# A buffer of their own for added pieces, and a first residual spread over four pieces, in a macaron encoder block

## The chip, the cores and the metric

The kernel runs on 1 core of one Trainium2 chip. The metric is the device time of one execution in microseconds (us). Engines are named as in the profile: PE is TensorE (matmuls; PEld its weight loads), DVE is VectorE, ACT is ScalarE, POOL is GpSimd, SP is SyncE, which here only issues DMA transfers.

## The reference

One layer on 256 tokens of width 2048, all in float32; every norm is an RMS norm.

```python
x = x + 0.5 * swiglu(rms_norm(x, ffn1_norm), ffn1_w_up, ffn1_w_down)
h = rms_norm(x, mix_norm)
proj = h @ w_in            # HGRN2 q, f, i, g; RG-LRU branch and gate; two branch gates
...                        # y_a: chunked gated recurrence; y_b: conv(4), RG-LRU scan, gelu gate
x = x + (g_a * (y_a @ w_branch_a) + g_b * (y_b @ w_branch_b)) @ w_out
x = x + cross_attention(rms_norm(x, xattn_norm), rms_norm(mem, mem_norm), wq, wkv, wo)
x = x + 0.5 * swiglu(rms_norm(x, ffn2_norm), ffn2_w_up, ffn2_w_down)
return rms_norm(x, final_norm)

def swiglu(h, w_up, w_down):
    gate, up = jnp.split(h @ w_up, 2, axis=-1)     # w_up is 2048 x 11264, w_down 5632 x 2048
    return (jax.nn.silu(gate) * up) @ w_down
```

## The kernel before

All weights stream through SBUF once, in pieces of 128 x 2048 float32 (1 MB). A piece is loaded into a buffer `raw`, then split into a high part `h` (ACT rounds it to fp32r, line 120) and a low part `l` (DVE subtracts, line 121), so that each float32 product becomes three fp32r products of high and low parts: two lines of PE (449 and 450) with `h`, one (452) with `l`. `raw`, `h` and `l` have three buffers each.

The two feed-forward layers (`ffn1`, `ffn2`) go through 11 groups of 512 hidden columns, each in 8 up pieces `wu` (p0 to p7), with the down pieces `wd` between. `ffn_order()` sets the order. Up pieces come in three kinds. *Plain*: load and split. *Fast*: seven products in place of eight; DVE forms differences `td` of the piece's columns (lines 213 to 215), and these are split too (`h<-td`, `tl`). *Mixed*: eight products, split like a plain one, but from (group 3, p6) on as an *added* piece: `begin_added` loads it (line 190), ACT writes its negative copy to `l` (line 191), and a DMA from POOL's queue adds `raw` to `l` in place (line 192); later `prepare` writes `h` (line 200). This spares DVE the subtraction. Group 3 (order p1, p3, p0, p4, p2, p6, p5, p7) has one added piece, groups 4 to 10 have two each, so each layer has 15.

`weights()` walks one plan of all pieces and prepares two pieces ahead of the products. A buffer of a pool is written again only when its last reader is done, and SP's queue is first in, first out: a load that waits for a free `raw` buffer holds back all loads behind it. A scheduler of the framework places instructions on each engine by its own estimate of times, except on SP, ACT and DVE during the first eight pieces, where the program's order is kept (`in_turn`); loads may be hoisted ahead when their buffer is free.

At the start (pieces 0 to 7 of `ffn1`, group 0), `head` and `rest` hang small steps on the pieces: `head_x(p)` loads an eighth of x by features (`xf`), scales it (`xg`) and splits it (`xh`, `xl`); `head_residual` loads the residual `x` by tokens and takes its squares (`TokenSquares.add`, ACT, line 352, into a scratch tile `junk`); `head_rstd` forms the root and its reciprocal `rtok`, then calls Silu once so that its table is loaded; `sums1` forms sums and differences `xs` of `xg` that the fast and mixed products need as operands, and splits them (`xd`, `xh`). The first products are scaled by `rtok` in `ev` when group 0 ends.

The pool `raw` serves plain, fast and added pieces alike:

```python
def begin_added(src):
    raw = rawp.tile([P, 2048], F32, name="raw", tag="raw")
    l = lp.tile([P, 2048], F32R, name="l", tag="l")
    sp.dma_start(raw, src)
    act.activation(l, raw, ACT.Copy, scale=-1.0)
    nc.gpsimd.dma_start(l, raw, accum_op=ALU.add)
```

Of the kernel before, what the change touches and what calls it, by code (L numbers as in the profile page):

```python
# [8 lines left out]
F32 = mybir.dt.float32  # L9
# [4 lines left out]
P = 128  # L14
T = 256
# [46 lines left out]
def block_kernel(ctx: ExitStack, tc: tile.TileContext, xT, xin, memT, vec, gfin, bgate, lruw, wu1, wd1, win, wv,  # L62
                 wg, wab, wout, wq, wk, wvm, wo, wu2, wd2, out_):
    nc = tc.nc
    pe, dve, act, sp = nc.tensor, nc.vector, nc.scalar, nc.sync

    def pool(name, bufs, **kw):
        return ctx.enter_context(tc.tile_pool(name=name, bufs=bufs, **kw))

    const = pool("const", 1)  # L70
    rawp = pool("raw", 3)
# [3 lines left out]
    small = pool("small", 2)  # L75
    psum = pool("psum", 8, space=bass.MemoryType.PSUM)
    scoped = {}

    @contextmanager
    def scope(**pools):  # L80
        with ExitStack() as inner:
            for name, bufs in pools.items():
                scoped[name] = inner.enter_context(tc.tile_pool(name=name, bufs=bufs, reuse_waits="tile"))
            yield
            scoped.clear()
# [4 lines left out]
    def t1(name="t1"):  # L90
        return scoped["tmp"].tile([P, T], F32, name=name, tag="t1")

    def bank(name="acc"):
        return psum.tile([P, 512], F32, name=name, tag="acc")
# [17 lines left out]
    xt = [const.tile([P, 4 * T], F32, name=f"x{q}") for q in range(4)]  # L112
# [48 lines left out]
    head, rest = [], {}  # L161
# [3 lines left out]
    def weights(*key):  # L165
        while plan and len(ahead) < 2:
            i = next(planned)
            k, src, kind = plan.pop(0)
            if i == 0:
                in_turn.enter_context(tc.manual_schedule(engines={sp.engine, act.engine, dve.engine}))  # L170
            if i < len(head):
                head[i]()
            if plan and plan[0][2] == "added":
                begun.append(begin_added(plan[0][1]))
            ahead.append((k, prepare(src, kind, 4 if i < 4 else 1)))
            if i in rest:
                rest[i]()
            if i == 7:
                in_turn.close()
        k, w = ahead.pop(0)  # L180
        assert k == key, (k, key)
        return w
# [2 lines left out]

    def begin_added(src):

        raw = rawp.tile([P, 2048], F32, name="raw", tag="raw")
        l = lp.tile([P, 2048], F32R, name="l", tag="l")
        sp.dma_start(raw, src)  # L190
        act.activation(l, raw, ACT.Copy, scale=-1.0)
        nc.gpsimd.dma_start(l, raw, accum_op=ALU.add)
        return raw, l
# [77 lines left out]
    class Operands:  # L271
# [13 lines left out]
        def add(self, src, gain=None):  # L285
            t = self.new()
            if gain is None:
                act.activation(t[:, :T], src, ACT.Copy)
                dve.tensor_tensor(out=t[:, T:], in0=src, in1=t[:, :T].bitcast(F32), op=ALU.subtract)
            else:  # L290
                act.activation(t[:, :T], src, ACT.Copy, scale=gain)
                dve.scalar_tensor_tensor(out=t[:, T:], in0=src, scalar=gain, in1=t[:, :T].bitcast(F32),  # L292
                                         op0=ALU.mult, op1=ALU.subtract)
            return t
# [10 lines left out]
    class Squares:  # L305
# [2 lines left out]

        def add(self, src):
            if self.ss is None:  # L310
                self.ss = small.tile([P, T], F32, name="ss", tag="ss")
                act.activation(self.ss, src, ACT.Square)
            else:
                s = t1("sq")
                act.activation(s, src, ACT.Square)
                dve.tensor_tensor(out=self.ss, in0=self.ss, in1=s, op=ALU.add)

        def rstd(self):

            acc = bank()  # L320
            pe.matmul(acc[:, :T], ones, self.ss, start=True, stop=True)
            std = t1("std")
            act.activation(std, acc[:, :T], ACT.Sqrt, bias=eps, scale=1.0 / D)
            r = small.tile([P, T], F32, name="rstd", tag="rstd", bufs=3)
            dve.reciprocal(out=r, in_=std)
            return r

# [9 lines left out]
            return r  # L337


    FFN_POOLS = dict(wide=3, hd=1)  # L340

    class TokenSquares:

# [3 lines left out]

        def add(self, c, ts=range(2)):
            for t in ts:
                name = "hd" if "hd" in scoped else "tmp2"  # L350
                junk = scoped[name].tile([P, 512], F32, name="junk", tag=name)
                act.activation(junk, xt[c][:, t * 512:(t + 1) * 512], ACT.Square,
                               accum_out=self.ss[:, t * 4 + c:t * 4 + c + 1])

# [17 lines left out]
    def by_feature(r):  # L372

        diag = t1("diag")
        for t in range(2):
            dve.tensor_scalar(out=diag[:, t * P:(t + 1) * P], in0=ident, scalar1=r[:, t:t + 1], scalar2=None,
                              op0=ALU.mult)
        acc = bank()
        pe.matmul(acc[:, :T], ones, diag, start=True, stop=True)
        o = small.tile([P, T], F32, name="rstd", tag="rstd", bufs=3)  # L380
        act.activation(o, acc[:, :T], ACT.Copy)
        return o

# [187 lines left out]
    pairs1, sq1 = [], TokenSquares()  # L571
# [3 lines left out]
    def head_x(p):  # L575

        q = p // 2
        if p % 2 == 0:
            xq[q] = slot(name="xf"), slot(name="xg"), []
        src, xg, out = xq[q]  # L580
        a = p % 2 * 512
        sp.dma_start(src[:, a:a + 512], xT[:, p * 512:(p + 1) * 512])
        sums = operand_pairs([src[:, a:a + 512]], "ffn1_norm", q, xg, out)
        if p % 2:
            sums1.append(sums)
        pairs1.append(out[-1])

    def head_residual(i):
        for c in (2 * i, 2 * i + 1):
            for t in range(2):  # L590
                sp.dma_start(xt[c][:, t * 512:(t + 1) * 512], xin[t * P:(t + 1) * P, c * 512:(c + 1) * 512])
            sq1.add(c)
        if i:
            sp.dma_start(vt[:, small_n:NVEC], vec[:, small_n:])

    head += [lambda p=p: head_x(p) for p in range(8)]
    for i in range(2):
        rest[4 + i] = lambda i=i: head_residual(i)
    rstd1 = []

    def head_rstd():
        rstd1.append(sq1.rstd_tokens())
        act.activation(rstd1[0][:, 2:], rstd1[0][:, :1], ACT.Silu)

    for q, i in enumerate((3, 6, 7, 9)):
        rest[i] = lambda q=q: sums1[q](((0, "less"), (1, "sums")))
    rest[8] = head_rstd
    for q, i in ((1, 17), (2, 18)):
        rest[i] = lambda q=q: sums1[q](((0, "sums"),))

# [49 lines left out]

    with scope(**FFN_POOLS):
        ffn("ffn1", pairs1, sq1, to_mix, rstds=rstd1)

    middle = ExitStack()
    middle.enter_context(scope(tmp=8, tmp2=2, scores=1, extra=2))

    xs = xs2.tiles
    side = []
# [18 lines left out]
    def proj(i):  # L687
        acc = product(xs, weights("in", i), late2)
        if not rs:
            rs["t"] = sq2.rstd_tokens()  # L690
            rs["f"] = by_feature(rs["t"])
        return acc
# [280 lines left out]
    for m in range(KT):  # L973
        acc = product(xs3.tiles, weights("q", m), late)
        if m == 0:
            rstd = by_feature(sq3.rstd_tokens())
            dve.tensor_scalar(out=rstd, in0=rstd, scalar1=HD ** -0.5, scalar2=None, op0=ALU.mult)
        qs.add(summed(acc, by=rstd))
        for i in range(2 * m, 2 * m + 2) if m < 4 else (m + 4,) if m < 12 else ():
            if i % 4 == 0:  # L980
                mt = slot(name="mem")
                sp.dma_start(mt, memT[:, i * T:(i + 4) * T])
            mk = heads(mt)[:, i % 4]
            ms.add(mk, col("mem_norm", i))
            sqm.add(mk)
# [41 lines left out]
    for g in range(4):  # L1027
# [4 lines left out]
        for t in range(2):  # L1032
            s = slot(F32R, "vs")
            f = scoped["tmp2"].tile([P, 512], F32, name="vf", tag="part")
# [58 lines left out]

    with scope(**FFN_POOLS):
        ffn("ffn2", pairs2, sq4, to_out, late, sums2)
# [93 lines left out]
```

## Time and profile before

| what | value |
|---|---|
| median of 3 runs | 2455.01 us (2454.0 to 2455.87) |
| the profiled execution | 2456.57 us, span 2454.8 us |
| granted PE clock, mean | 0.997 |
| PE busy | 2434.6 us (99%), 12250 matmuls |
| DVE, ACT, POOL busy | 1894.1, 1391.2, 28.3 us |
| DMA | 507.59 MB, mean 207 GB/s |
| loads of one piece, issue to landing | 4.8 us, median of 172 up pieces |
| adding transfers on POOL's queue | 30, 7.3 us, median |

A row of a timeline gives start and duration in us, engine and line, the operation, the tiles as out<-in without buffer numbers, their shapes, how many were merged, and in brackets how long the engine had been idle and what ended that. Matmuls overlap: a row lasts 0.39 us and the next starts 0.23 us later. A windows row gives each engine's busy time in a stretch, the share of the clock that PE was granted, and what the DMA engines did.

### The profile page before, as it was taken

To read this page: it belongs to the slowest core of one execution; us is meant where nothing else is said; L and a number is where in the kernel's file an instruction comes from. 1 tells how busy PE (TensorE), PEld (TensorE's weight loads), DVE (VectorE), ACT (ScalarE), POOL (GpSimd) and SP (SyncE) were. 2 spreads that over 40 slices of the span, in tenths; PEclk is the share of its full clock that TensorE was granted. 3 is DMA by queue.
4 is the path that set the end of the run, shared out by engine and by line. 5 is a ranking of instruction groups with operands and counts; after the bars stand their busy time and mean duration, and the time that the engine had idled before them with its cause. 6 is when DMAs were issued, how large, how long until landed. Compare 5 with 4: busy or idle time off the path is not lost.

```text
span 2454.8 us, 30191 instructions
## 1 busy us (share of the span) xinstructions
PE 2434.6 (99%) x12250; PEld 2036.9 (83%) x12250; DVE 1894.1 (77%) x2016; ACT 1391.2 (57%) x1398; POOL 28.3 (1%) x36
## 2 busy tenths in 40 slices
PE   9999999999999999999999999999999999999998
PEld 7887888888888888888888888888888788888887
DVE  6998999999865757567665676556689999999995
ACT  7555666666564454477434554555555566666664
POOL 0000000000000000000000000000000000000000
PEclk9999999999999999999999999999999999999999
DMA  7557777777655445546555555444555677777774
GB/s 278 190 203 234 248 235 235 234 239 239 223 183 194 173 172 180 174 166 228 194 188 177 210 198 189 172 172 155 189 189 189 209 238 239 240 240 235 235 235 152
DMA packets 75020, 507.59 MB, mean 207 GB/s; under 512 B 8320, under 2 KB 8576, under 8 KB 15232
## 3 DMA queue, kind: packets, MB, share of 16 engines
q1 hardware_dynamic: 69840, 473.06, 53.4%
q0 software_dynamic: 4320, 31.46, 6.4%
q8 instruction: 96, 1.57, 0.2%
q10 hardware_dynamic: 720, 1.13, 0.1%
q14 instruction: 44, 0.36, 0.0%
HBM read 472.07 MB, written 2.10 MB: 193 GB/s over the span
## 4 chain that ended last, share of the span: by engine, by line
PE 95%; DVE 2%; ACT 1%; DMA 1%; issue 0%; SPq 0%; ACTq 0%; DVEq 0%
PE acc L449 17%; PE acc L450 17%; PE acc L452 17%; PE acc L231 11%; PE acc L252 8%; PE acc L253 8%; PE acc L255 8%; PE acc L235 5%; DMA raw<-wu 1%; PE acc L489 1%; ACT h L120 1%; DVE l L121 1%; PE acc L389 1%; PE acc L765 0%; PE acc L1048 0%; PE acc L1003 0%
## 5 line engine op out<-in xcount | busy, mean ns | idle before, releaser
L121 DVE TENSOR_TENSOR l<-raw,h 128x2048 fp32r<-128x2048 f32 (+2 forms) x422 | 878.0, 2087 | 364.5 <-ACT h L120 353.0
L120 ACT ACTIVATE h<-raw 128x2048 fp32r<-128x2048 f32 (+2 forms) x422 | 736.7, 1753 | 637.5 <-PE acc L253 204.8
L449 PE MATMUL acc<-h,xh 128*128 128x512 f32 x1280 | 501.2, 392 | 7.1 <-ACT h L120 7.0
L450 PE MATMUL acc<-h,xl 128*128 128x512 f32 x1280 | 499.7, 391 | 0.0
L120 ACT ACTIVATE h<-td 128x1024 fp32r<-128x1024 f32 x224 | 229.6, 1055 | 178.4 <-PE acc L450 131.0
L252 PE MATMUL acc<-h,ops 128*128 128x512 f32 x832 | 326.9, 393 | 0.0
L253 PE MATMUL acc<-h,ops 128*128 128x512 f32 x832 | 324.3, 390 | 0.0
L121 DVE TENSOR_TENSOR tl<-td,h 128x1024 fp32r<-128x1024 f32 x224 | 267.4, 1221 | 33.6 <-ACT h L120 31.0
L449 PEld LDWEIGHTS acc<-h,xh 128*128 128x128 f32 x1280 | 241.7, 189 | 60.0 <-ACT h L120 9.7
L450 PEld LDWEIGHTS acc<-h,xl 128*128 128x128 f32 x1280 | 241.9, 189 | 50.1
L231 PE MATMUL acc<-ops,h 128*128 128x512 f32 x1152 | 278.0, 393 | 0.3
L449 PE MATMUL acc<-h,hidop 128*128 128x512 f32 x704 | 275.7, 392 | 0.0
L450 PE MATMUL acc<-h,hidop 128*128 128x512 f32 x704 | 274.3, 390 | 0.0
L231 PEld LDWEIGHTS acc<-ops,h 128*128 128x128 f32 x1152 | 211.9, 188 | 42.9 <-DVE ops L292 0.9
L452 PE MATMUL acc<-l,xh 128*128 128x512 f32 x832 | 218.9, 390 | 0.0
L255 PE MATMUL acc<-l,ops 128*128 128x512 f32 x832 | 206.1, 390 | 0.0
L452 PE MATMUL acc<-l,hidop 128*128 128x512 f32 x704 | 188.3, 389 | 0.0
L452 PEld LDWEIGHTS acc<-l,xh 128*128 128x128 f32 x832 | 156.5, 188 | 32.6
L255 PEld LDWEIGHTS acc<-l,ops 128*128 128x128 f32 x832 | 156.2, 188 | 32.4
L252 PEld LDWEIGHTS acc<-h,ops 128*128 128x128 f32 x832 | 156.2, 188 | 32.3
L253 PEld LDWEIGHTS acc<-h,ops 128*128 128x128 f32 x832 | 156.3, 188 | 31.6
L452 PEld LDWEIGHTS acc<-l,hidop 128*128 128x128 f32 x704 | 132.2, 188 | 27.5
(220 smaller groups left out, 2347.6 us busy)
## 6 DMA issues: line engine op xcount, KB each, us to landing
raw<-wu SPq DMA_DIRECT2D x172, 1024.0 KB, 4.8
raw<-wd SPq DMA_DIRECT2D x88, 1024.0 KB, 4.8
raw<-win SPq DMA_DIRECT2D x40, 1024.0 KB, 4.8
raw<-wg SPq DMA_DIRECT2D x32, 1024.0 KB, 4.8
l<-raw POOLq DMA_DIRECT2D x30, 1024.0 KB, 7.3
raw<-wab SPq DMA_DIRECT2D x16, 1024.0 KB, 4.8
raw<-wout SPq DMA_DIRECT2D x16, 1024.0 KB, 4.8
raw<-wq SPq DMA_DIRECT2D x16, 1024.0 KB, 4.8
```

Source lines behind the costliest of these rows:

```text
L120: done["high"] = act.activation(h, raw, ACT.Copy).ins
L121: dve.tensor_tensor(out=l, in0=raw, in1=h.bitcast(F32), op=ALU.subtract)
L231: pe.matmul(acc, h[:, k * P:(k + 1) * P], xs[k], start=k == 0, stop=False)
L235: done["product"] = pe.matmul(acc[:, :T], l[:, k * P:(k + 1) * P], xs[k][:, :T], start=False, stop=k == KT - 1).ins
L252: pe.matmul(accs[t], x[:, t * P:][:, :P], h[j], start=first and j == 0, stop=False)
L253: pe.matmul(accs[t], x[:, T + t * P:][:, :P], h[j], start=False, stop=False)
L255: done["product"] = pe.matmul(accs[t], x[:, t * P:][:, :P], l[j], start=False, stop=last and j == 3).ins
L389: pe.transpose(accs[m // 2][:, m % 2 * T + t * P:][:, :P], tile[:, t * 512 + m * P:][:, :P], ident)
L449: pe.matmul(acc, ah, bh, start=start, stop=False)
L450: pe.matmul(acc, al, bh, start=False, stop=False)
L452: pe.matmul(acc, ah, bl, start=False, stop=stop)
L489: pe.transpose(acc[:, z * T + t * P:][:, :P], hid[t][:, (2 * y + z) * P:][:, :P], ident)
```

## The change

Four things change. `begin_added` loads into a tile `own` of a pool with one buffer (8 KB a partition), in place of one of the three `raw` buffers. For its space the scratch `hd` goes (the squares of the feed-forward layers write their `junk` into a `wide` tile), and `rstd` and `ss` move from `small` to a pool `feature` that lives only in the middle of the program. The first residual's loads and squares, two of its four quarters behind each of pieces 4 and 5 before, now come one quarter behind each of pieces 4, 5, 6 and 7. And `head_rstd` moves from behind the last of them to the next piece, with the sums around it moved by a piece or so. Core of the diff:

```diff
     def begin_added(src):
-        raw = rawp.tile([P, 2048], F32, name="raw", tag="raw")
+        raw = scoped["own"].tile([P, 2048], F32, name="own", tag="own")
...
-                self.ss = small.tile([P, T], F32, name="ss", tag="ss")
+                self.ss = scoped["feature"].tile([P, T], F32, name="ss", tag="ss", bufs=1)
...
-            r = small.tile([P, T], F32, name="rstd", tag="rstd", bufs=3)
+            r = scoped["feature"].tile([P, T], F32, name="rstd", tag="rstd")
...
-    FFN_POOLS = dict(wide=3, hd=1)
+    FFN_POOLS = dict(wide=3, own=1)
...
-                name = "hd" if "hd" in scoped else "tmp2"
-                junk = scoped[name].tile([P, 512], F32, name="junk", tag=name)
+                if "wide" in scoped:
+                    junk = scoped["wide"].tile([P, 2048], F32, name="junk", tag="wide")[:, :512]
+                else:
+                    junk = scoped["tmp2"].tile([P, 512], F32, name="junk", tag="tmp2")
...
-    def head_residual(i):
-        for c in (2 * i, 2 * i + 1):
-            for t in range(2):
-                sp.dma_start(xt[c][:, t * 512:(t + 1) * 512], xin[t * P:(t + 1) * P, c * 512:(c + 1) * 512])
-            sq1.add(c)
-        if i:
+    def head_residual(c):
+        for t in range(2):
+            sp.dma_start(xt[c][:, t * 512:(t + 1) * 512], xin[t * P:(t + 1) * P, c * 512:(c + 1) * 512])
+        sq1.add(c)
+        if c == 3:
             sp.dma_start(vt[:, small_n:NVEC], vec[:, small_n:])
...
-    for i in range(2):
-        rest[4 + i] = lambda i=i: head_residual(i)
...
-    for q, i in enumerate((3, 6, 7, 9)):
+    for i in range(3):
+        rest[4 + i] = lambda i=i: head_residual(i)
+    for q, i in enumerate((3, 7, 8, 9)):
         rest[i] = lambda q=q: sums1[q](((0, "less"), (1, "sums")))
-    rest[8] = head_rstd
+    made = rest[7], rest[8]
+    rest[7] = lambda: [f() for f in (lambda: head_residual(3), made[0])]
+    rest[8] = lambda: [f() for f in (head_rstd, made[1])]
...
-    middle.enter_context(scope(tmp=8, tmp2=2, scores=1, extra=2))
+    middle.enter_context(scope(tmp=8, tmp2=2, scores=1, extra=2, feature=3))
```

The first place is ACT's queue from the split of piece 5 (the first `h<-raw` row) to the first `ev`. `x_100`, `x_101` and `x_102` are quarters of the residual, `stdt` the root, `rtok` its reciprocal. Before:

```order
L120 ACTIVATE h<-raw 128x2048
L352 ACTIVATE junk,sst<-x_101 128x512 x2
L352 ACTIVATE junk,sst<-x_102 128x512 x2
L412 ACTIVATE xg<-xf,vt 128x256 x2
L362 ACT_TABLE_LOAD
L362 ACTIVATE stdt<-stdt,eps 128x2
L120 ACTIVATE xh<-xg 128x512
L603 ACT_TABLE_LOAD
L603 ACTIVATE rtok<-rtok 128x1
L120 ACTIVATE h<-raw 128x2048
```

And now, the split of piece 7 first, and between two such splits ahead of it only a pair of squares, `xg` and `xh`:

```order
L120 ACTIVATE h<-raw 128x2048
L354 ACTIVATE junk,sst<-x_102 128x512 x2
L120 ACTIVATE xd<-xs 128x256
L364 ACT_TABLE_LOAD
L364 ACTIVATE stdt<-stdt,eps 128x2
L120 ACTIVATE h<-raw 128x2048
L120 ACTIVATE xh<-xs 128x512
L602 ACT_TABLE_LOAD
L602 ACTIVATE rtok<-rtok 128x1
L120 ACTIVATE xd<-xs 128x256
L120 ACTIVATE xh<-xs 128x512
L483 ACTIVATE ev<-acc,rtok 128x512 x2
```

The two table loads have moved from ahead of the split of piece 6 to both sides of the split of piece 8, directly ahead of the first `ev`.

The second place is SP's queue at the start of the program (`xf` and `raw<-wu` are the loads of pieces 0, 1, 2 and so on, piece 2 being the third pair of rows). Before:

```order
L582 DMA xf<-xT 128x512
L207 DMA raw<-wu 128x512 x4
L582 DMA xf<-xT 128x512
L207 DMA raw<-wu 128x512 x4
L582 DMA xf<-xT 128x512
L207 DMA raw<-wu 128x512 x4
```

And now:

```order
L584 DMA xf<-xT 128x512
L207 DMA raw<-wu 128x512 x4
L584 DMA xf<-xT 128x512
L207 DMA raw<-wu 128x512 x4
L190 DMA own<-wu 128x2048
L584 DMA xf<-xT 128x512
L207 DMA raw<-wu 128x512 x4
```

The load of group 3's added piece has moved to the third place of the program, ahead of piece 2; in the same way the second layer's first one now stands among the loads of the cross-attention's value weights.

The third place is SP's queue from group 3's p0 to group 5 of the first layer; line 190 is an added piece's load, 210 a fast one's, 207 a plain one's or a down piece's. Before:

```order
L207 DMA raw<-wu 128x2048
L210 DMA raw<-wu 128x2048
L190 DMA raw<-wu 128x2048
L210 DMA raw<-wu 128x2048 x3
L207 DMA raw<-wd 128x2048 x4
L210 DMA raw<-wu 128x2048
L190 DMA raw<-wu 128x2048
L210 DMA raw<-wu 128x2048 x2
L190 DMA raw<-wu 128x2048
L210 DMA raw<-wu 128x2048 x3
```

And now:

```order
L207 DMA raw<-wu 128x2048
L210 DMA raw<-wu 128x2048 x4
L190 DMA own<-wu 128x2048
L207 DMA raw<-wd 128x2048 x4
L210 DMA raw<-wu 128x2048 x5
L190 DMA own<-wu 128x2048
L210 DMA raw<-wu 128x2048
L207 DMA raw<-wd 128x2048
L190 DMA own<-wu 128x2048
```

Group 3's four fast loads now stand in a row, and from group 4 on the first added piece of a group is loaded before the down pieces ahead of it, the second behind the group's fifth fast load.

More of the change, by code (lines that the diff above doesn't have):

```diff
@@ L379, in by_feature @@
         pe.matmul(acc[:, :T], ones, diag, start=True, stop=True)
-        o = small.tile([P, T], F32, name="rstd", tag="rstd", bufs=3)
+        o = scoped["feature"].tile([P, T], F32, name="rstd", tag="rstd")
         act.activation(o, acc[:, :T], ACT.Copy)
```

## The prediction

> **What bounds the kernel now.** I read the page first, then busy time in stretches (the windows view), then TensorE's timeline where a stretch had idle time, then the timelines of ScalarE (ACT), VectorE (DVE) and the load queue (SP) just ahead of each gap.
>
> ```profile
> span 2454.8 us, 30191 instructions
> PE 2434.6 (99%) x12250; PEld 2036.9 (83%) x12250; DVE 1894.1 (77%) x2016; ACT 1391.2 (57%) x1398; POOL 28.3 (1%) x36
> ```
>
> TensorE is busy for 2434.6 of 2454.8 us and the change takes no matmul away. So what can be won is idle time, 20.2 us, and what a half clock costs. The windows view tells where they lie (its columns: busy time and count of each engine, granted clock, DMA share, GB/s):
>
> ```profile
> core 0: us, PE busy (x) PEld busy (x) DVE busy (x) ACT busy (x) POOL busy (x), PEclk, DMA share, GB/s
> 6.00:32.00 26.00, 25.97 (x118) 21.46 (x117) 18.50 (x31) 22.61 (x44) 0.00 (x0) 1.00 1.03 392
> 0.00:39.00 39.00, 37.91 (x175) 32.20 (x176) 21.52 (x36) 32.71 (x64) 0.20 (x4) 1.00 0.94 353
> 39.00:52.00 13.00, 9.33 (x33) 6.93 (x32) 7.28 (x12) 8.77 (x10) 0.00 (x0) 0.87 0.24 90
> 60.00:160.00 100.00, 100.00 (x450) 82.66 (x448) 99.47 (x109) 56.71 (x49) 0.00 (x0) 1.00 0.55 200
> 182.00:197.00 15.00, 11.63 (x42) 8.49 (x41) 11.67 (x12) 8.33 (x7) 0.00 (x0) 0.89 0.82 270
> 197.00:700.00 503.00, 503.00 (x2260) 416.91 (x2259) 453.95 (x457) 306.51 (x260) 13.12 (x15) 1.00 0.71 232
> 1924.00:1934.00 10.00, 6.97 (x24) 5.23 (x23) 8.06 (x8) 3.68 (x4) 0.00 (x0) 0.83 0.66 256
> 2440.00:2455.00 15.00, 6.05 (x27) 4.69 (x25) 4.23 (x10) 4.70 (x10) 0.00 (x0) 0.79 0.36 140
> ```
>
> Three short stretches hold what a change could take. Idle time plus the share of clock not granted: 39 to 52 us, 3.67 + 0.13 x 13 = 5.4; 182 to 197, 3.37 + 0.11 x 15 = 5.0; 1924 to 1934, 3.03 + 0.17 x 10 = 4.7. Together 15.1 us. The last row is the tail behind the last product (8.95 us idle) and is not touched; the start has 1.1 us. The long stretches have none: 197 to 700 is busy to the last hundredth. TensorE's timeline names what ended each gap (start, duration, engine, line, tiles, idle before and its releaser):
>
> ```profile
> 17.67 0.39 PE L449 MATMUL acc<-h,xh 128*128 128x512 f32 x1
> 23.11 0.39 PE L449 MATMUL acc<-h,xh 128*128 128x512 f32 x1
> 42.09 0.66 PE L449 MATMUL acc<-h,xh 128*128 128x512 f32 x1 [2.50 <-ACT h L120]
> 50.59 0.50 PE L449 MATMUL acc<-h,xh 128*128 128x512 f32 x1 [1.17 <-ACT h L120]
> 191.41 0.50 PE L449 MATMUL acc<-h,xh 128*128 128x512 f32 x1 [3.02 <-ACT h L120]
> 1928.36 0.73 PE L452 MATMUL acc<-tl,xh 128*128 128x512 f32 x2 [3.03 <-DVE tl L121]
> ```
>
> The first two rows are the starts of pieces 2 and 3 (I count the first eight loads 0 to 7): TensorE takes 5.44 us for a piece. In all four gaps TensorE waits for a split, not for its own work.
>
> **Term 1, the head (39 to 52 us).** ACT ahead of the first gap (the splits of pieces 4, 5 and 6 are the first, second and last of its rows), then DVE's low part of piece 6:
>
> ```profile
> 24.87 1.90 ACT L120 ACTIVATE h<-raw 128x2048 fp32r<-128x2048 f32 x1
> ...
> 31.02 1.91 ACT L120 ACTIVATE h<-raw 128x2048 fp32r<-128x2048 f32 x1
> 32.83 0.61 ACT L352 ACTIVATE junk<-x 128x512 f32<-128x512 f32 x1
> 35.70 0.90 ACT L412 ACTIVATE xg<-xf,vt 128x256 f32<-128x256 f32 x2
> 36.61 1.28 ACT L362 ACT_TABLE_LOAD   x1
> 37.91 0.29 ACT L362 ACTIVATE stdt<-stdt,eps 128x2 f32<-128x2 f32 x1
> 38.11 0.62 ACT L120 ACTIVATE xh<-xg 128x512 fp32r<-128x512 f32 x1
> 38.74 1.28 ACT L603 ACT_TABLE_LOAD   x1
> 40.04 0.20 ACT L603 ACTIVATE rtok<-rtok 128x1 f32<-128x1 f32 x1
> 40.15 1.89 ACT L120 ACTIVATE h<-raw 128x2048 fp32r<-128x2048 f32 x1
> 42.07 2.29 DVE L121 TENSOR_TENSOR l<-raw,h 128x2048 fp32r<-128x2048 f32 x1 [2.62 <-ACT h L120]
> ```
>
> From split to split ACT needs 40.15 - 31.02 = 9.13 us, against TensorE's 5.44. Four squares take 2.87 of them (32.83 to 35.70), the two table loads with their root and Silu 3.05. In the new order only two squares stand between two splits: 1.91 + 1.44 + 0.90 + 0.62 = 4.9 us, under 5.44. So pieces 4 to 7 no longer fall behind, and both gaps (2.50 and 1.17, and the half clock behind the first) go.
>
> What is added there: the first transfer of `own`, 1.05 MB, now stands on SP's queue ahead of piece 2. The DMA is saturated then (share 1.03, 392 GB/s from 6 to 32 us), so everything behind it lands 1.05 / 0.392 = 2.7 us later; a load alone has 4.8 us from issue to landing in the page, the upper bound. Two residual transfers (0.52 MB, 1.3 us) are taken out ahead of piece 5 and four ahead of piece 6, so from piece 6 on the delay is made up. Each piece then brings 1.05 + 0.26 + 0.52 MB = 4.7 us of stream, under 5.44. I allow 0.5 us of new stall at piece 2 or 4, which is lost only if nothing later is late anyway.
>
> What is late next: the roots. Their tables now come behind the squares of piece 7. The split of piece 4 began at 24.87; with between none and all of the 2.7 us passed on to it I take 26.0, so an end at 27.9. Three more rounds of 4.9 us end the split of piece 7 at 42.6. Then come two squares and `xd`, which waits for DVE's low part of piece 7 (2.29) and two sums: it ends at about 45.8. Table, root and split of piece 8 (3.5): 49.3, just ahead of TensorE, which without its gaps wants piece 8 at 23.11 + 5 x 5.44 = 50.3. Two operand copies before and two behind the second table and the Silu, about 3.2 in all: 52.5. The first `ev` could start at 50.3 and waits 2.2 us. The Trainium skill (ScalarE: Activation LUTs, What ACT_TABLE_LOAD costs) adds a drain of about 1.4 us to each such load. This case's trace disagrees: the root starts 0.02 us after the load. By the page's rule the `ev` would come 2.8 us later still, and an estimate of the whole gain by it would be 10.2 us.
>
> DVE then sets the pace: from 60 to 160 us it is busy 99.47 of 100 us, and the sums of three quarters of x now stand in a row ahead of its low part of piece 8. TensorE can only start group 1 earlier by as much as DVE does. So I keep 4.0 of the 5.4 us; bounds 1.5 (DVE moves forward only by what the sums leave) and 5.4.
>
> **Term 2, group 3 of the first layer (182 to 197 us).** SP's issues, and the chain of waits in both layers:
>
> ```profile
> 159.97 0.33 SPq L210 DMA_DIRECT2D raw<-wu  x1
> 169.41 0.33 SPq L190 DMA_DIRECT2D raw<-wu  x1
> 175.62 12.67 SPq L210 DMA_DIRECT2D raw<-wu  x3
> ...
> 178.49 10.33 DMA raw<-wu
> 1915.19 10.65 DMA raw<-wu
> ```
>
> At 169.41 a free `raw` buffer goes to the first added piece (L190); the two fast pieces behind it issue at 175.62 and 178.49, the latter beside the adding transfer, and the chain runs through its 10.33 us. In the new order these two take the places of 169.41 and 175.62, 6.2 and 2.9 us earlier, and the second is under way before the adding transfer reads. The gap of 3.02 us goes, and its half clock. The added piece's own chain doesn't get later: its data lies in `own` since the start. DVE may still be late by some tenths: 4.5 of 5.0, bounds 0 and 5.0.
>
> The Trainium skill (DMA: Bandwidth & Descriptors, Issuing engines are not separate DMA queues) speaks against the change: transfers of the GpSimd and SyncE queues run on the same engines, so a buffer of its own takes no contention away. The trace agrees (10.33 us beside the adding transfer). By that rule alone an estimate of terms 2 and 3 is nothing; rival B prices it from rows.
>
> **Term 3, group 3 of the second layer (1924 to 1934 us).** The same mechanism, 10.65 us, gap 3.03. The first `own` transfer is issued in the cross-attention stage, where TensorE is busy throughout. 4.5 of 4.7, bounds 0 and 4.7.
>
> **Term 4, the steady groups: a wait is added.** With one `own` buffer, a group's second added load waits until the first one's copy (L200) and adding transfer have read it. One group before:
>
> ```profile
> 286.88 1.90 ACT L191 ACTIVATE l<-raw 128x2048 fp32r<-128x2048 f32 x1
> 296.42 1.91 ACT L200 ACTIVATE h<-raw 128x2048 fp32r<-128x2048 f32 x1
> 303.00 1.91 ACT L191 ACTIVATE l<-raw 128x2048 fp32r<-128x2048 f32 x1
> 306.30 1.49 ACT L120 ACTIVATE h<-raw 128x1536 fp32r<-128x1536 f32 x1 [1.40 <-PE acc L450]
> 312.62 0.39 PE L449 MATMUL acc<-h,xh 128*128 128x512 f32 x1
> DMA to landing us min/median/max: 7.1/7.3/11.4
> DMA to landing us min/median/max: 4.6/5.1/7.1
> ```
>
> The last two rows are the adding transfers (L192) and the loads of added pieces (L190). L200 ends at 298.33; a load of 5.1 us lands at 303.4, where ACT now starts the negative copy at 303.00: 0.4 us late, 2.4 with the longest load. In-order behind it on ACT stands the split of 306.30, for which TensorE comes at 312.62, 4.8 us after its end; on SP stand one up and one down load. The cost is nothing as long as the delay stays under 1.40 + 4.8 us; beyond, every group pays.
>
> The rest costs nothing: squares write into `wide` in place of `hd` on the same engine, small tiles move to another pool, no instruction is added.
>
> **Sum.** 4.0 + 4.5 + 4.5 = 13.0 us off the profiled execution of 2456.57 us (span 2454.8 and 1.8 around it): 2443.6. That execution is 1.6 above the median of 2455.01, so I forecast 2442.0 us.
>
> **Rivals.** A: DVE eats the head. It is at 99.47% behind it, and its order has the sums bunched; then only 1.5 us of term 1 stays (10.5 in all): 2444.5 us; at the worst none (9.0), 2446.0. B: the contention moves. The third fast load of group 3 now runs beside the adding transfer and takes the 10.3 us; if that is needed at once, terms 2 and 3 are lost: 2455.0 - 4.0 = 2451.0. Against it: it is needed a piece later, 5 us. C, slower: the single buffer throttles the groups. For it: one load in turn with one adding transfer. It decides from 6.2 us of delay on. Against it: the longest adding transfer and the longest load in a row put the negative copy at 286.88 + 1.90 + 11.4 + 7.1 = 307.3, 4.3 us late; it takes 2 us more than any row shows. At 2 us of gap in each of the 14 groups that hold two added pieces it costs 28, less the 13.0 won: 2470 us. D: new stalls in the head, from `own` ahead of piece 2 and the roots behind piece 8, give back what the three places win; 4.8 + 2.2 us and two half-clock spells of 1.7 are 10.4 of 13.0: 2452.4, no change by the measure below.
>
> **Chances.** Forecast 0.60, A 0.14, B 0.09, C 0.10, D 0.07. About 0.2% (4.9 us) is what a measurement of this kernel can tell from no change. Faster: forecast, A and half of B (2451.0 lies a us off the edge of 2450.1): 0.79. Same: the other half of B, and D: 0.11. Slower: C, 0.10. The range holds forecast, A and B: from all 15.1 us and 2 us for gaps that the stretches round away (2438) to B's 2451 with a us to spare (2452).
>
> **What would show it.** Right: ACT's split of piece 6 within 5 us of that of piece 5; the table loads behind four pairs of squares; none of TensorE's four gaps left, shifted by the gain, and clock 1.00 there. The gap of the first `ev` at about 2 us, DVE full from 45 us. SP: loads of 4.8 us at group 3. Wrong: ACT waiting for `own` in every group, or TensorE's gaps at the same places with another releaser.

## Result, and the profile after

The changed kernel takes 2442.17 us (median of 4 runs, 2441.86 to 2442.53) against 2454.93 before (4 runs, 2454.0 to 2455.87): ratio 0.9945, 95% interval 0.9933 to 0.9958. 2442.0 was forecast. The profiled execution is one of 2442.24 us.

The page and the stretches of the prediction, now of the kernel after:

```profile
span 2440.5 us, 30183 instructions
PE 2430.0 (100%) x12250; PEld 2033.8 (83%) x12250; DVE 1892.8 (78%) x2016; ACT 1390.8 (57%) x1398; POOL 28.3 (1%) x36
```

```profile
core 0: us, PE busy (x) PEld busy (x) DVE busy (x) ACT busy (x) POOL busy (x), PEclk, DMA share, GB/s
...
39.00:52.00 13.00, 13.00 (x59) 10.78 (x58) 11.38 (x26) 11.37 (x19) 0.00 (x0) 1.00 0.65 233
60.00:160.00 100.00, 99.87 (x441) 81.16 (x440) 97.92 (x104) 56.27 (x47) 0.00 (x0) 1.00 0.57 209
182.00:197.00 15.00, 15.00 (x68) 12.41 (x67) 15.00 (x15) 9.37 (x9) 0.00 (x0) 1.00 0.74 261
197.00:700.00 503.00, 503.00 (x2264) 416.77 (x2263) 451.55 (x457) 307.90 (x265) 12.14 (x14) 1.00 0.70 232
1924.00:1934.00 10.00, 10.00 (x46) 8.29 (x45) 9.14 (x7) 7.20 (x5) 0.00 (x0) 1.00 0.66 224
```

The three stretches with idle time are full at clock 1.00, and nothing opened in the long one where the wait was added. All waits of TensorE that the profile shows are now these (in total, times, longest):

```profile
PE warm L109 <- DVE ones L106: 1.1, 1, 1.1
PE acc L451 <- ACT h L120: 0.3, 1, 0.3
```

A stretch shifted by the gain is a poor measure, so I follow fixed points of TensorE's program instead: the transposes of a group's hidden rows, which stand at the start of group 3 and of group 4. The view of the tile `ev` gives count, duration (least, median, most) and, after the colon, when they run. Before, then after; in each, group 3 and 4 of the first layer, then of the second:

```profile
L489 PE MATMUL acc<-vt,ev x4: 270/272/272, 166.3 to 166.7; 128*128 128x128 f32 x4
L489 PE MATMUL acc<-vt,ev x6: 271/272/273, 224.4 to 225.0; 128*128 128x128 f32 x6
L489 PE MATMUL acc<-vt,ev x4: 270/272/272, 1904.4 to 1904.7; 128*128 128x128 f32 x4
L489 PE MATMUL acc<-vt,ev x6: 270/272/273, 1961.4 to 1961.9; 128*128 128x128 f32 x6
```

```profile
L491 PE MATMUL acc<-vt,ev x4: 270/272/272, 162.7 to 163.0; 128*128 128x128 f32 x4
L491 PE MATMUL acc<-vt,ev x8: 270/272/273, 215.1 to 215.9; 128*128 128x128 f32 x8
L491 PE MATMUL acc<-vt,ev x4: 270/272/273, 1894.9 to 1895.3; 128*128 128x128 f32 x4
L491 PE MATMUL acc<-vt,ev x8: 271/272/273, 1947.0 to 1947.8; 128*128 128x128 f32 x8
```

Head: group 3 is entered at 162.7 in place of 166.3, 3.6 us. Group 3 of the first layer takes 52.4 us in place of 58.1, 5.7; of the second layer 52.1 in place of 57.0, 4.9. Together 14.2 of the 14.3 us by which the span is shorter; the rest of the program moved by 0.1.

ScalarE in the head, after (the four splits are those of pieces 4 to 7):

```profile
27.36 1.90 ACT L120 ACTIVATE h<-raw 128x2048 fp32r<-128x2048 f32 x1
...
31.86 1.90 ACT L120 ACTIVATE h<-raw 128x2048 fp32r<-128x2048 f32 x1
...
36.35 1.91 ACT L120 ACTIVATE h<-raw 128x2048 fp32r<-128x2048 f32 x1
...
40.84 1.90 ACT L120 ACTIVATE h<-raw 128x2048 fp32r<-128x2048 f32 x1
...
45.94 1.28 ACT L364 ACT_TABLE_LOAD   x1
47.23 0.30 ACT L364 ACTIVATE stdt<-stdt,eps 128x2 f32<-128x2 f32 x1
47.44 1.90 ACT L120 ACTIVATE h<-raw 128x2048 fp32r<-128x2048 f32 x1
...
52.11 1.24 ACT L483 ACTIVATE ev<-acc,rtok 128x512 f32<-128x512 f32 x2
```

The splits come every 4.5 us, where 9.13 lay between those of pieces 5 and 6; the first table load stands behind all squares, ahead of piece 8's split, and the first `ev` comes at 52.1.

### The profile page after: what moved, and what is told of

Same layout as the page of the kernel before. It is cut to its first block, busy times and chain, and to the rows that moved or that the text cites. A ratio compares the mean times of both kernels' runs of the same rounds, so it can differ in the third digit from the quotient of the medians.

```text
span 2440.5 us, 30183 instructions
## 1 busy us (share of the span) xinstructions
PE 2430.0 (100%) x12250; PEld 2033.8 (83%) x12250; DVE 1892.8 (78%) x2016; ACT 1390.8 (57%) x1398; POOL 28.3 (1%) x36
## 4 chain that ended last, share of the span: by engine, by line
PE 97%; DVE 1%; ACT 1%; DMA 1%; issue 0%; SPq 0%; ACTq 0%; DVEq 0%
PE acc L451 18%; PE acc L454 18%; PE acc L452 18%; PE acc L231 11%; PE acc L252 8%; PE acc L253 8%; PE acc L255 8%; PE acc L235 6%; PE acc L491 1%; PE acc L391 1%; ACT h L120 0%; PE acc L768 0%; DVE l L121 0%; DMA xf<-xT 0%; PE acc L1051 0%; PE acc L1006 0%
```

## The experiments

Each ratio is against the kernel before on the same chip beside the run (its median there: 2456.07 us beside e1 to e4, 2455.95 beside e5 to e8, 2455.57 beside e9 to e11); "group 3 at" is the entry into group 3 of the first layer, read as above. Some expectations read it at a neighbouring row: 0.2 to 0.3 us earlier in e9 and e10, 1.8 us later in e3.

| run | us (range) | ratio, 95% interval | group 3 at |
|---|---|---|---|
| before | 2454.93 | 1 | 166.3 |
| after | 2442.17 (2441.86–2442.53) | 0.9945, 0.9933–0.9958 | 162.7 |
| e1 own buffer only | 2447.99 (2447.29–2449.47) | 0.9966, 0.9954–0.9979 | 167.8 |
| e2 head only | 2451.59 (2449.02–2452.38) | 0.9981, 0.9972–0.9989 | 162.0 |
| e3 after, own's first load late | 2442.08 (2441.83–2442.41) | 0.9942, 0.9929–0.9954 | 162.6 |
| e4 after, four shared buffers | 2441.21 (2440.92–2442.1) | 0.9939, 0.9926–0.9953 | 161.9 |
| e5 before, no adding transfer at group 3 | 2446.07 (2445.64–2447.3) | 0.9960, 0.9946–0.9974 | 166.1 |
| e6 after, own loaded twice | 2459.5 (2454.35–2465.0) | 1.0019, 1.0009–1.0028 | 167.5 |
| e7 after, own loaded three times | 2541.05 (2536.31–2545.25) | 1.0344, 1.0328–1.0361 | 167.3 |
| e8 e4 and four early added pieces | 2439.49 (2439.4–2439.68) | 0.9932, 0.9919–0.9945 | 160.6 |
| e9 before, roots late | 2451.15 (2449.7–2452.78) | 0.9983, 0.9974–0.9991 | 162.5 |
| e10 e1, own's first load late | 2446.32 (2446.04–2446.4) | 0.9962, 0.9949–0.9974 | 166.8 |
| e11 after and four early added pieces | 2440.83 (2440.49–2441.34) | 0.9940, 0.9927–0.9954 | 161.8 |

### The two halves apart: e1 and e2

e1 is the kernel after with the order of the head of before; e2 has the new head, and its added pieces take their buffers from the shared three. In both, as in all runs but e5, squares and small tiles lie where the kernel after has them:

```
e1:  head_residual, rest, sums of the kernel before
e2: -        raw = scoped["own"].tile([P, 2048], F32, name="own", tag="own")
    +        raw = rawp.tile([P, 2048], F32, name="raw", tag="raw")
```

> The buffer of its own alone; the head is that of the kernel before (two squares of 128x512 behind each of four residual loads stand in pairs of quarters behind pieces 4 and 5). Theory (the parts are independent, and in the trace after group 3 gave 5.7 us in the first layer and 4.9 in the second, the head 3.6): 2454.9 - 10.6 = 2444.3 us; TensorE has no wait at group 3 in either layer, the waits of 2.5 and 1.2 us near 42 and 50 us stay. Rival, contention alone (a load beside the adding transfer takes 10.3 us wherever it is issued): the waits of 3.0 us at group 3 stay and the time is 2454.9 us. Rival, own's load ahead of piece 2 harms the old head too: 0.7 to 2.7 us more, 2445.0 to 2447.0 us.

> The new head alone; added pieces load into the three shared buffers as before. Theory (independent parts): 2454.9 - 3.6 = 2451.3 us, 2450.6 if the 0.66 us lost at piece 4 goes too (no load of 1 MB stands ahead of piece 2 here); the waits of about 3.0 us at group 3 of both layers stay. Rival, the head's gain is lost again at the next wait (what ends group 3's wait is set by transfers that don't come earlier): 2454.9 us, with a longer wait at group 3.

e1's entries into groups 3 and 4, and TensorE's waits in its head:

```profile
L491 PE MATMUL acc<-vt,ev x4: 270/272/273, 167.8 to 168.1; 128*128 128x128 f32 x4
L491 PE MATMUL acc<-vt,ev x8: 271/272/273, 220.2 to 220.9; 128*128 128x128 f32 x8
```

```profile
43.46 0.79 PE L451 MATMUL acc<-h,xh 128*128 128x512 f32 x1 [2.96 <-ACT h L120]
51.96 0.50 PE L451 MATMUL acc<-h,xh 128*128 128x512 f32 x1 [1.18 <-ACT h L120]
```

Group 3 takes the 52.4 us of the kernel after, with no wait left in either layer: contention alone, the rival, is out. But the head is 1.5 us worse than before (167.8 against 166.3), with the same two waits, the first 0.46 longer, which is a third of it. So by the trace the buffer alone is worth 5.7 + 4.9 - 1.5 = 9.1 us, and 8.1 by the medians, not 10.6: the harm rival, which allowed 7.9 to 9.9.

e2, the same points and its waits at group 3 of both layers:

```profile
L491 PE MATMUL acc<-vt,ev x4: 270/272/272, 162.0 to 162.4; 128*128 128x128 f32 x4
L491 PE MATMUL acc<-vt,ev x8: 271/272/273, 221.6 to 222.4; 128*128 128x128 f32 x8
```

```profile
187.36 0.79 PE L451 MATMUL acc<-h,xh 128*128 128x512 f32 x1 [3.02 <-ACT h L120]
...
1924.92 0.50 PE L454 MATMUL acc<-tl,xh 128*128 128x512 f32 x1 [2.48 <-DVE tl L121]
```

Without own's load in the first transfers the new head is worth 4.3 us; of the 4.3, own takes 0.7 back in the kernel after. Group 3 of the first layer then took 59.6 us, 1.5 longer than before. That is not the rival's longer wait, for the wait is 3.02 us as before. It is mostly the clock behind it:

```profile
176.00:195.00 19.00, 15.36 (x53) 11.51 (x52) 13.46 (x13) 8.96 (x8) 0.00 (x0) 0.82 0.86 276
```

Here 0.18 x 19 = 3.4 us were not granted, twice the 0.11 x 15 = 1.7 of the kernel before (182 to 197 us). In the second layer the wait was 2.48 us in place of 3.03 and the clock stayed at 1.00 behind it, so that group 3 took 54.9 us in place of 57.0. That the sum comes out as the theory had it (2451.59, 2451.3 expected) is thus in part luck: 0.7 more in the head, 1.5 lost and 2.1 won at group 3. By the medians the halves are worth 8.1 and 4.5 us, 12.6 together; as one change 12.8 by the medians, 13.5 by the ratio. They add up, though the clock shifted about 2 us from place to place.

### What own's first load costs: e3 and e10

```
e3 and e10, first added piece only:
-        sp.dma_start(raw, src)
+        with tc.issue_after(loads[7]):
+            sp.dma_start(raw, src)
```

e3 is otherwise the kernel after, e10 otherwise e1.

> As the kernel after, but the first load into own is issued behind piece 7's and 8's loads and no longer ahead of piece 2's. Theory, VectorE sets the head's end (it is busy 97.9 of 100 us from 60 to 160): the slip of 0.66 us at piece 4 goes, the small slips between 58 and 77 us (2.1 us in all) grow by as much, and group 3 is entered at 164.5 us as in the kernel after: 2442.2 us. Rival, the stall at piece 4 is paid in full: group 3 is entered at 163.9, 2441.5 us. The difference is under what the times tell, so the trace of TensorE decides.

> As the run with the buffer of its own alone, but own's first load is issued behind the loads of pieces 7 and 8. Theory: own's load ahead of piece 2 is what cost the old head 1.43 us there (group 3 entered at 167.55 us, 166.12 before); group 3 is entered at 166.1, 2448.0 - 1.4 = 2446.6 us. Rival, it is something else of the change in the head (squares written into a wide buffer): 167.5 and 2448.0 us.

e10: 166.8 in place of e1's 167.8, 2446.32 us. So the place of that load is what hurt the old head, for 1.0 of the 1.5 us; the other 0.5 stays open.

e3's number came out as the theory had it, its mechanism did not. Group 3 is entered at 162.6, though TensorE no longer waits at piece 4. But the small slips between 58 and 77 us did not grow: what was won went in one place, most of it in a wait of 0.41 us at 89 us, behind two splits that waited for loads (ScalarE's rows of e3):

```profile
84.05 1.92 ACT L120 ACTIVATE h<-raw 128x2048 fp32r<-128x2048 f32 x1 [0.95 <-DMA raw<-wu]
...
86.52 1.92 ACT L120 ACTIVATE h<-raw 128x2048 fp32r<-128x2048 f32 x1 [0.55 <-DMA raw<-wd]
```

The two loads were issued 0.9 us earlier than in the kernel after (77.52 and 79.68 us), but took 6.4 and 6.7 us, 4.9 and 5.4 there. Own's load had gone out 35 us before them, so that it was late doesn't explain this; the cause is open. What the load ahead of piece 2 costs the new head is read from e2 instead, 0.7 us; e3 says nothing on VectorE. That needed e8.

### Which part of the new head counts: e9

The kernel before, with its residual in pairs of quarters; the roots are held behind piece 8's split:

```
-    rest[8] = head_rstd
+    def roots_late():
+        with tc.issue_after(done["high"]):
+            head_rstd()
+    rest[8] = roots_late
```

> The kernel before (three shared buffers, squares of two quarters behind each of pieces 4 and 5), with the root, the Silu and so their two table loads issued behind the split of piece 8. It parts the new head into its two effects. Theory, ScalarE's row of 9.13 us between the splits of pieces 5 and 6 is what counts: without the 3.05 us of the tables 6.1 are left, the split of piece 6 ends at about 39.0 us, where TensorE wants it at 39.6: no wait at 39 to 42 us, and group 3 is entered at 161.8 to 163 us as with the whole new head (161.8; before 166.1): 2451 to 2452 us. Rival, the squares in pairs of quarters delay pieces 6 and 7 by themselves: a wait of 1 us or more stays there, group 3 is entered at 164 or later, 2453 us or more. Rival, the first ev, now some 4.5 us behind the last product of group 0, stalls TensorE in place of the wait removed: 2453 us, with a wait released by ev.

```profile
46.74 0.50 PE L451 MATMUL acc<-h,xh 128*128 128x512 f32 x1 [1.44 <-ACT h L120]
```

```profile
39.00:52.00 13.00, 11.56 (x51) 9.21 (x50) 9.91 (x16) 9.54 (x12) 0.00 (x0) 1.00 0.38 125
```

The wait of 2.50 us at piece 6 and the half clock behind it are gone, one of 1.44 at piece 7 is left (the first rival's wait, but not its time), and group 3 is entered at 162.5: 3.8 of the new head's 4.3 us. No `ev` stalls TensorE. So the table loads' place is nearly all of it, and the spread of the squares, which is what moved them, adds 0.5. Of the 3.8, 1.7 are the half clock.

### Contention, and one buffer more: e5 and e4

e5 is the kernel before without the adding transfer (L192) of the first added piece of each layer, whose low part is then left uncorrected. e4 gives the kernel after one rotation of four buffers for every load of the layers:

```
e5: +        if len(begins) not in (1, 16):
             nc.gpsimd.dma_start(l, raw, accum_op=ALU.add)
e4: +    def raw_tile():
    +        turns.append(0)
    +        if len(turns) % 4 == 0:
    +            return scoped["own"].tile([P, 2048], F32, name="own", tag="own")
    +        return rawp.tile([P, 2048], F32, name="raw", tag="raw")
```

> The kernel before, without the adding transfer of the first added piece of each layer (that piece's low part is left uncorrected, so this run computes less). Theory, contention: the fast load that is issued at 178.5 us takes 10.3 us because the adding transfer runs beside it; without it the load takes about 5 us, lands 5 us earlier, which is more than the wait of 3.0: no wait at group 3 in either layer, 2455 - (5.0 + 4.7) = 2445.3 us. Rival, lateness of the buffer alone: a load that is issued 9 us later than in the kernel after is too late in any case; the waits of 3.0 us stay, 2455 us. Between: part of the wait stays, too short for the clock to fall, 2447 to 2450 us.

> As the kernel after, but the eighth KB of a partition that own takes serve as a fourth buffer in one rotation of four for all of the layers' loads, added pieces among them. Theory, what counts is that the two fast loads of group 3 find a buffer before the adding transfer runs: a fourth shared buffer does the same, no wait at group 3, and no added piece waits for own: 2442.2 us, to 2441.5 with piece 4's slip gone. Rival, only the buffer set apart takes the added load out of the fast loads' way: here the added load still stands ahead of two fast loads, the second of them runs beside the adding transfer for 10.3 us, one wait of up to 3 us at group 3 of each layer stays: 2442.2 + 2 x 4.9 = 2452 us.

The third of group 3's four fast loads, which before was issued at 178.49 us and took 10.33 (the DMA view: engine and queue, count, size, us to landing), in e5, issued at 178.20:

```profile
raw<-wu SPq DMA_DIRECT2D x1, 1024.0 KB, 4.7
```

The same one in e4, issued at 166.94, and the fourth, issued at 172.80:

```profile
raw<-wu SPq DMA_DIRECT2D x1, 1024.0 KB, 4.8
```

```profile
own<-wu SPq DMA_DIRECT2D x1, 1024.0 KB, 6.8
```

Taking the neighbour away halves the load with the same buffers at the same time, and both waits go (2446.07, 2445.3 expected): the contention is real. In e4 the added load still stands ahead of three fast loads, and its adding transfer runs beside the fourth, which takes 6.8 us; but TensorE doesn't wait, since group 3 is entered 4.4 us earlier and the third load is issued 11.6 us earlier than before, 7.2 by TensorE's own program. What counts is thus that the fast loads find a buffer soon; that the added load's is set apart is not needed. e4, which has no early load of an added piece either, is 0.9 us under e3 beside it on the same chip, but their ranges overlap by 0.3.

### How much slack the added wait has: e6 and e7

```
         sp.dma_start(raw, src)
+        for _ in range(1):          # e7: range(2)
+            nc.gpsimd.dma_start(raw, src)
         act.activation(l, raw, ACT.Copy, scale=-1.0)
```

> The kernel after, with each load into own done twice, the second behind the first on GpSimd's queue, so that the negative copy waits about 5 to 6 us more; all else is as it was. It tests the slack of 6.2 us (1.4 + 4.8) of the second added piece of a group, of which the kernel after uses 0.4 to 2.1. Theory: the copy comes 5.4 to 8.1 us late, up to 1.9 us over the slack in some of the 14 groups: 2442 to 2455 us, 2447 the likeliest. Rival, no slack behind ScalarE's row (each delay is paid): 14 x 5.5 = 77 us more, 2519 us. Rival, far more slack than ScalarE's row shows: 2442 us, no wait of TensorE.

> As the run with own loaded twice, but three times: the copy comes 10 to 14 us late. Theory, slack 6.2 us: 4 to 8 us over it in 14 groups, 56 to 112 us more, 2500 to 2555 us, with TensorE waiting once in each group. Rival, each delay is paid: 14 x 11 = 154 more, 2596 us. Rival, far more slack: below 2450 us.

The negative copies of the kernel after: all 30 (busy time, mean ns, idle time just before them and its cause), and the two of group 4, where ScalarE waited longest. Behind them one group of e6 with TensorE's wait, and e6's longest wait:

```profile
L191 ACT ACTIVATE l<-own 128x2048 fp32r<-128x2048 f32 x30 | 57.3, 1910 | 13.8 <-DMA own<-wu 13.8
```

```profile
215.42 1.90 ACT L191 ACTIVATE l<-own 128x2048 fp32r<-128x2048 f32 x1
...
236.23 1.92 ACT L191 ACTIVATE l<-own 128x2048 fp32r<-128x2048 f32 x1 [3.29 <-DMA own<-wu]
```

```profile
408.95 1.90 ACT L193 ACTIVATE l<-own 128x2048 fp32r<-128x2048 f32 x1
...
434.35 1.92 ACT L193 ACTIVATE l<-own 128x2048 fp32r<-128x2048 f32 x1 [4.49 <-DMA own<-wu]
```

```profile
437.26 0.50 PE L453 MATMUL acc<-h,xh 128*128 128x512 f32 x1 [1.04 <-ACT h L120]
...
32.44 0.50 PE L453 MATMUL acc<-h,xh 128*128 128x512 f32 x1 [3.13 <-ACT h L120]
```

Before, the two copies lie 16.12 us apart (286.88 to 303.00). In the kernel after the second is 4.7 us late in group 4 (20.81 apart), 0.4 to 2.1 in the 13 others, and TensorE waits in none. In e6 they lie 25.4 apart here, 9.3 late, and TensorE waits; over its 14 groups the copy is 7.2 to 10.1 us late, 8.3 on average.

e6 loses 17.3 us against the kernel after, but not all of it in the groups. Its longest wait, 3.13 us, lies in the head, where own's first load is doubled too, and group 3 is entered 4.8 us later (167.5 in place of 162.7). That leaves 12.5 us, and TensorE's waits in the groups are 11.9 us, 0.2 to 1.3 each, in 11 of the 14; three groups (7.2, 7.8 and 8.2 us late) have none. The theory's 2447 was too low because it left the head out, and because the second load, issued on GpSimd behind the first, brought more than the 5.4 to 8.1 us allowed for. e7's waits of TensorE:

```profile
PE acc L456 <- DMA l<-own: 37.2, 13, 3.7
PE acc L453 <- ACT h L202: 32.4, 14, 6.1
```

One or two in each of the 14 groups, and 81.5 us more than e6, 5.8 for each group. The copy is 13.3 us late on average, 5.0 more than in e6, and the waits grow by 4.2 us a group; the rest is for the most part clock (0.992 granted in place of 0.998). So beyond the point nearly each us is paid. 4.7 us late costs nothing, and from 7.2 us on most groups lose something. With 11.9 us lost in 14 groups at 8.3 us late, the point lies near 7.5 us (an estimate); 6.2 was predicted.

### VectorE as the head's limit: e8 and e11

Four mixed pieces of groups 1 and 2 are made as added pieces, in e8 with e4's four buffers, in e11 with `own`:

```
+EARLY = ((1, 2), (1, 6), (2, 2), (2, 6))
-  "added" if e[0] == "mixed" and e[1:] > (3, 0) else "plain"
+  "added" if e[0] == "mixed" and (e[1:] > (3, 0) or e[1:] in EARLY) else "plain"
```

> The kernel with four shared buffers, and four mixed pieces of groups 1 and 2 (the third and last mixed pieces in order of each, numbers 2 and 6) made as added pieces: VectorE loses four passes of 2.29 us, ScalarE gets four copies of 1.91 us, four adding transfers more. Theory, VectorE limits what the new head can bring (small slips of TensorE between 57 and 76 us, 2.1 us in all): most of them go, group 3 is entered 1.3 to 2.1 us earlier, 2439.1 to 2439.9 us. Rival, the adding transfers slow the fast loads beside them (10.3 us for one at group 3 of the kernel before): new waits of TensorE of up to 3 us in groups 1 and 2, 2444 us or more. Rival, the slips are not VectorE's: 2441.2 us.

> The kernel after with the same four mixed pieces of groups 1 and 2 made as added pieces, but with the buffer set apart for added pieces and not the rotation of four. Theory, VectorE's relief is worth the same there: 2442.2 - 1.7 = 2440.5 us. Rival, with one buffer set apart the added pieces of groups 1 and 2 follow each other too closely (25 us apart; load, copy and adding transfer take about 5 + 2 + 8 to 11): ScalarE waits and TensorE with it, 2442 us or more.

e4 and then e8 behind the head:

```profile
60.00:160.00 100.00, 99.87 (x440) 81.05 (x439) 98.68 (x104) 55.79 (x47) 0.00 (x0) 1.00 0.57 210
60.00:160.00 100.00, 100.00 (x446) 82.56 (x445) 90.85 (x99) 61.59 (x51) 2.61 (x3) 1.00 0.72 243
```

VectorE is busy 90.85 of 100 us in place of 98.68, group 3 is entered at 160.6 in place of e4's 161.9, and the time is 2439.49, 1.7 less than e4's; e11 gains 0.9 at group 3 and 1.3 in all over the kernel after. VectorE's passes were what held TensorE there. The added transfers in groups 1 and 2 brought no wait in e8; e11 has one of 0.3 us at 62 us. e8 is the fastest kernel of this study, 2.7 us below the kernel after.

## Why the prediction was right, by its steps

**Ceiling.** The three stretches were rated at 15.1 us; 14.2 came. Group 3's 5.0 was itself exceeded: 5.7. The other 0.7 is in neither the idle time nor the clock of that stretch; about 0.4 of it shows in TensorE's rows from 181 to 188 us, which follow each other less closely than after, and the rest was not isolated.

**Term 1, the head: 4.0 forecast, 3.6 measured.** The row of 9.13 us was the cause. e9 shows which half of it: the tables' 3.05 us, not the squares' 2.87. The prediction gave both and weighed neither. Of the 3.6 us, 1.7 are the half clock behind the first wait. Its 4.9 us from split to split came as 4.5: I added durations, but neighbouring rows of ScalarE overlap by about 0.1 (a pair of squares takes 1.23 us from start to start, not 1.44). The chain of the roots was close: `xd` to 45.92, the split of piece 8 to 49.34, first `ev` at 52.11 (45.8, 49.3, 52.5 forecast). That was luck in part: piece 4's split began at 27.36 and not at 26.0, 2.5 of own's 2.7 us passed on, and the shorter rounds made up for it. The `ev` was 0.9 us behind group 0's end, not 2.2, for TensorE came to piece 8 at 51.22 and not at 50.3; it waited nowhere for it. The Trainium skill (ScalarE: Activation LUTs, What ACT_TABLE_LOAD costs) would have added 1.38 us of drain to each load; the trace disagrees, for the root starts 47.23 - 45.94 - 1.28 = 0.01 us after it. Own's load ahead of piece 2 cost 0.7 (e2 against after), 0.5 allowed. That VectorE takes the rest was right: e8 wins 1.3 us there by relieving it alone.

**Term 2, group 3 of the first layer: 4.5 forecast, 5.7 measured.** Mechanism as stated; the third and fourth fast load after, issued at 171.99 and 174.86 us:

```profile
raw<-wu SPq DMA_DIRECT2D x1, 1024.0 KB, 4.7
```

```profile
raw<-wu SPq DMA_DIRECT2D x1, 1024.0 KB, 5.4
```

The third comes 2.9 us earlier by TensorE's program (6.5 with the head's 3.6), ahead of the adding transfer of 176.19. Rival B's load beside that transfer, the fourth, takes 5.4 and not 10.3. The mis-sized term is the gap: 0.5 was held back for a late VectorE, and no such wait came, and the ceiling was 0.7 too low. The Trainium skill's rule that queues of different engines share the same DMA engines (DMA: Bandwidth & Descriptors, Issuing engines are not separate DMA queues) is borne out by e5; what it doesn't weigh is when a transfer starts, and that decided.

**Term 3, the second layer: 4.5 forecast, 4.9 measured.** Same mechanism. Its size holds 1.7 us of half clock, which does not follow each such wait (last section).

**Term 4, the steady groups: nothing forecast, nothing measured.** The copy was 0.4 to 2.1 us late in 13 groups, as named (0.4 to 2.4), and 4.7 in one, which lies beyond even rival C's worst case of 4.3; TensorE waited in none.

**The rest.** The sum was 13.0 off the profiled execution; 14.3 came, from 2456.57 to 2442.24. By the medians it is 12.8: before's profiled execution lay 1.6 above its median, after's 0.1. So the forecast hit the median more closely than its terms hit theirs, by luck: the terms were 1.2 us short together, and the profiled execution's excess of 1.6 went the other way. What the other runs of before had less of is not known. Rival A holds in part (VectorE kept 1.3 us of the head, e8); D's stalls in the head came to 0.7.

## What to carry to other kernels

When a busy engine waits at a few places only, look at what stands in the other engine's row just ahead of each: two table loads in the wrong place cost more here than four squares. A transfer slowed by a neighbour can be started earlier rather than kept apart from it, and a fourth buffer in the common rotation did that as well as one reserved. Price a new wait by how late its work may be; the slack read off ScalarE's row (6.2 us) was about right (near 7.5 by the runs), and past it nearly each us was paid in every group.

## What the hardware showed that was not expected

The length of a wait did not decide whether the clock fell behind it. In e5 a wait of 2.23 us in the head was followed by 3.4 us of half clock (0.13 x 13 = 1.7 us not granted; products of TensorE followed each other every 0.43 us in place of 0.23). In e9 one of 2.54 us at group 3 of the second layer was followed by none, and in e7 not even one of 3.54 us (wait, then the stretch around it with the granted clock; e5, then e7):

```profile
41.80 0.78 PE L451 MATMUL acc<-h,xh 128*128 128x512 f32 x1 [2.23 <-ACT h L120]
...
39.00:52.00 13.00, 9.62 (x34) 7.19 (x33) 7.29 (x12) 8.77 (x11) 0.00 (x0) 0.87 0.22 83
```

```profile
605.29 2.11 PE L456 MATMUL acc<-l,xh 128*128 128x512 f32 x8 [3.54 <-DMA l<-own]
...
605.00:615.00 10.00, 9.71 (x43) 8.04 (x44) 5.83 (x6) 5.32 (x4) 0.55 (x1) 1.00 0.70 260
```

So a removed wait of 2 to 3 us is worth its length, or 1.7 us more (3.4 behind e2's of 3.02), and a trace with several such waits can differ by that from one variant to the next with no other cause to be seen in it.
